# A sparse 3x3 convolution: one more load up front, a first store that waits for loads, and 28 matmuls on zeros in place of 12

## The chip, the core and the metric

One core of one Trainium2 chip. The metric is device time in microseconds (us) of one execution. The kernel before takes 127.04 us (median of 3 runs, 126.94 to 127.04; its profiled run 127.33). The span in a profile, from the first to the last instruction, is about 1.7 us shorter than the time. Each run is sorted by state, fast or slow, and only fast runs are compared.

## The reference, cut to what matters

```python
# x: (16, 64, 64, 64) fp32, weight: (128, 64, 3, 3) fp32, 90% zeros; output: (16, 128, 64, 64) fp32
x_pad = np.pad(x, ((0, 0), (0, 0), (1, 1), (1, 1)), mode='constant')
for b, co, ci, kh, kw:                     # five nested loops
    if weight[co, ci, kh, kw] != 0:
        output[b, co] += weight[co, ci, kh, kw] * x_pad[b, ci, kh:kh+h, kw:kw+w]
```

Input x is 16.8 MB, the output is 33.6 MB, the weights are 0.3 MB.

## The kernel before

Two images form a pair: their 64 input channels each fill 128 partitions, and there are eight pairs. A pair's load casts fp32 to bf16 on the way and is issued from GpSimd; a pair's output goes out in two stores of 2 MB, issued from SyncE. The first half of pair 0 comes as fp32 and is cast on chip (the head). TensorE runs small matmuls on zeros while it has nothing else to do, so that its clock does not fall.

```python
    nc.sync.dma_start(out=w_sb, in_=weight.rearrange("o i kh kw -> o (i kh kw)"))
    x_head = o_pool.tile([128, H, W], FP32, name="o")
    nc.sync.dma_start(out=x_head[:, 0:HEAD, :], in_=pair(0)[:, 0:HEAD, :])
    nc.gpsimd.dma_start(out=xs[0][:, HEAD:H, :], in_=pair(0)[:, HEAD:H, :])
    ...                                              # (cut)
    EARLY = 4
    for p in range(1, EARLY):
        load(p)                                      # pairs 1, 2, 3 up front
    ...
    keep_busy(27)                                    # 128x128 matmuls on zeros
    ...                                              # casts and transposes of the weights
    keep_busy(12)
    ...
    for p in range(NP):
        o = [o_pool.tile([C_OUT, H, W], FP32, name="o") for _ in range(2)]
        for blk in range(4):
            ...                                      # 30 matmuls, 4 additions on VectorE, 2 copies on ScalarE
                if p > 0 and blk == 1 and p + EARLY - 1 < NP:
                    load(p + EARLY - 1)              # pairs 4 to 7
        if not last:
            for n in range(2):
                nc.sync.dma_start(out=out[2 * p + n], in_=o[n])
```

## Time and profile before

| what | kernel before |
|---|---|
| time, median | 127.04 us |
| span of the profiled run (127.33 us) | 125.6 us |
| first product of TensorE; last addition of VectorE ends | 7.43 us; 113.66 us |
| first store issued; pair 6's first store issued | 23.5 us; 100.3 us |
| the two data queues' packets | 97.0% of 16 engines' span |
| HBM traffic | 17.07 MB read, 33.55 MB written |

How to read it: the page divides the span into 40 slices of 3.14 us and gives the busy share of each engine in tenths.

### The profile page before, as it was taken

What the parts mean: (1) busy time and instruction counts of PE and PEld (TensorE: products, weight loads), DVE (VectorE), ACT (ScalarE), POOL (GpSimd) and SP (SyncE); (2) the same over time, 40 slices, a digit from 0 to 9 for tenths busy, and PEclk for the clock granted to TensorE, in tenths of its full rate; (3) what the DMA queues carried; (4) which work ended last, traced back from release to release, by engine and by line L of the source; (5) the groups of instructions that cost most, each with busy time, mean ns of one, the idle gap of its engine ahead of it and who ended that gap; (6) DMA issues with size and microseconds to landing.
All of it is one profiled execution on the core that took longest, in us unless ns stands there. A gap on an engine that the chain in (4) does not pass through costs nothing.

```text
span 125.6 us, 2510 instructions
## 1 busy us (share of the span) xinstructions
PE 109.4 (87%) x1014; PEld 56.1 (45%) x1014; DVE 82.3 (66%) x135; ACT 39.0 (31%) x71; POOL 40.6 (32%) x45
## 2 busy tenths in 40 slices
PE   6769999999999999999999999999999999970000
PEld 6624444545454545444554555455545555430000
DVE  0352477877787777888788878877877787772000
ACT  4541533333333333333333333333333333330000
POOL 6327353334433443334333333333333330000000
PEclk9967999999999999999999999999999999999555
DMA  4999999999999999999999999999999999999980
GB/s 119 361 230 214 214 209 219 217 157 399 423 334 305 303 433 311 344 308 407 342 305 329 397 428 444 418 420 423 438 428 444 418 423 423 433 405 423 431 373 26
DMA packets 4044, 42.93 MB, mean 342 GB/s; under 512 B 448, under 2 KB 448, under 8 KB 704
## 3 DMA queue, kind: packets, MB, share of 16 engines
q1 hardware_dynamic: 2880, 34.90, 66.1%
q0 software_dynamic: 1152, 7.86, 30.9%
q8 instruction: 8, 0.13, 0.4%
q14 instruction: 4, 0.03, 0.1%
HBM read 17.07 MB, written 33.55 MB: 403 GB/s over the span
## 4 chain that ended last, share of the span: by engine, by line
PE 83%; DMA 5%; DVE 1%; issue 1%; DVEq 0%; SPq 0%
PE ps L146 83%; DMA o<-in_x_dram 5%; DVE o L179 1%; DVEq L229 0%; DVE x L97 0%; SPq L60 0%; DVEq L179 0%
## 5 line engine op out<-in xcount | busy, mean ns | idle before, releaser
L179 DVE TENSOR_TENSOR o<-ps,pc 128x512 f32<-128x512 f32 x124 | 77.8, 686 | 22.1 <-PE ps L146 19.8
L146 PE MATMUL ps<-x,wT 64*128 64x504 bf16 (+3 forms) x780 | 90.1, 378 | 1.5 <-DVE x L97 1.5
L146 PEld LDWEIGHTS <-wT 64*128 64x128 bf16 x966 | 52.1, 95 | 54.0 <-issue 3.4
L165 POOL TENSOR_TENSOR s<-x 128x512 bf16<-128x512 bf16 x31 | 35.6, 1151 | 59.7 <-PE ps L146 43.3
L172 ACT COPY pc<-ps 128x512 f32<-128x512 f32 x62 | 33.3, 589 | 64.0 <-issue 61.8
L146 PE MATMUL ps<-s,wT 64*128 64x512 bf16 (+1 forms) x186 | 25.5, 377 | 0.0
L82 PE MATMUL ps<-idle_rhs 128*128 128x128 bf16 x39 | 3.9, 283 | 1.0 <-DVE idle_rhs L77 1.0
L82 PEld LDWEIGHTS <-idle_rhs 128*128 128x128 bf16 x39 | 3.5, 133 | 1.0 <-DVE idle_rhs L77 1.0
L68 POOL DMA_DIRECT2D x<-in_x_dram x7 | 3.9, 559 | 0.0
L160 DVE COPY o<-ps 128x512 f32<-128x512 f32 x2 | 1.4, 692 | 3.6 <-PE ps L146 3.6
L101 DVE CAST w_bf<-w_sb 128x192 bf16<-128x192 f32 (+1 forms) x4 | 1.1, 345 | 2.8 <-DMA w_sb<-in_weight_dram 2.8
L159 ACT COPY o<-ps 128x512 f32<-128x512 f32 x2 | 1.2, 586 | 4.0 <-PE ps L146 4.0
L97 ACT CAST x<-o 128x576 bf16<-128x576 f32 (+1 forms) x2 | 1.5, 802 | 1.2 <-DMA o<-in_x_dram 1.2
L97 DVE CAST x<-o 128x576 bf16<-128x576 f32 x1 | 0.5, 460 | 2.0 <-DMA o<-in_x_dram 2.0
L101 ACT ACT_TABLE_LOAD x1 | 1.3, 1283 | 0.7 <-PEq L218 0.7
L101 ACT CAST w_bf<-w_sb 128x64 bf16<-128x64 f32 (+1 forms) x2 | 0.7, 416 | 1.7 <-DMA w_sb<-in_weight_dram 1.7
L107 PE MATMUL ps<-ident,w_bf 128*128 128x128 bf16 x9 | 0.9, 222 | 0.3 <-DVE w_bf L101 0.3
L111 DVE TENSOR_TENSOR wT<-ps,wT 128x384 bf16<-128x384 f32 x2 | 1.0, 550 | 0.0
L63 POOL DMA_DIRECT2D x<-in_x_dram x1 | 0.7, 691 | 0.8 <-POOLq L218 0.8
L107 PEld LDWEIGHTS <-w_bf 128*128 128x128 bf16 x9 | 0.5, 97 | 0.8 <-DVE w_bf L101 0.7
L77 DVE MEMSET idle_rhs<- 128x64 uint32 x1 | 0.1, 112 | 0.8 <-PEq L218 0.8
L122 DVE CAST wT<-ps 128x384 bf16<-128x384 f32 x1 | 0.6, 552 | 0.0
(8 smaller groups left out, 1.9 us busy)
## 6 DMA issues: line engine op xcount, KB each, us to landing
out_dram<-o SPq DMA_DIRECT2D x14, 2048.0 KB, 16.9
x<-in_x_dram POOLq DMA_DIRECT2D x7, 1024.0 KB, 15.5
out_dram<-o SPq DMA_DIRECT2D x4, 1024.0 KB, 10.6
o<-in_x_dram SPq DMA_DIRECT2D x1, 1024.0 KB, 5.7
x<-in_x_dram POOLq DMA_DIRECT2D x1, 512.0 KB, 7.5
w_sb<-in_weight_dram SPq DMA_DIRECT2D x1, 288.0 KB, 3.0
```

Of the source, the lines that this page charges most:

```text
L68: nc.gpsimd.dma_start(out=xs[p], in_=pair(p))
L82: nc.tensor.matmul(idle_ps, idle_rhs, idle_rhs, start=True, stop=True)
L97: copy(out=xs[0][:, a:b, :], in_=x_head[:, a:b, :])
L101: copy(out=w_bf4[:, g, a:b, :], in_=w_v[:, k : k + b - a, :])
L107: nc.tensor.matmul(wps[:, j, :], src, ident, start=True, stop=True)
L111: nc.vector.tensor_tensor(out=wT[:, g], in0=wps, in1=wT[:, G1], op=SUB)
L146: nc.tensor.matmul(ps[n][:, lo:hi, c_lo:c_hi], tap(g, kw, n), src[q, a:b:step, c_lo + kw - 1 : c_hi + kw - 1], start=(i == 0), stop=(i == ...
L159: nc.scalar.copy(out=o[0][:, r0 : r0 + rows, :], in_=ps[0])
L160: nc.vector.tensor_copy(out=o[1][:, r0 : r0 + rows, :], in_=ps[1])
L165: nc.gpsimd.tensor_tensor(out=s, in0=xs[p][:, r0 : r0 + 16 : 2, :], in1=xs[p][:, r0 + 1 : r0 + 16 : 2, :], op=ADD)
L172: nc.scalar.copy(out=c, in_=shared[n])
L179: nc.vector.tensor_tensor(out=o[n][:, first : r0 + 16 : 2, :], in0=ps[n], in1=pc[n], op=ADD)
```

## The change

Its intent: have x on chip early, keep stores out of the way of the first loads, and close the pause of TensorE before the first products.

```diff
-    EARLY = 4
-    for p in range(1, EARLY):
-        load(p)
+    EARLY = 5
+    landed = [load(p) for p in range(1, EARLY)][-2]
 ...
-    keep_busy(12)
+    keep_busy(28)
 ...
-                if p > 0 and blk == 1 and p + EARLY - 1 < NP:
-                    load(p + EARLY - 1)
+                if p > 1 and blk == 1 and p + EARLY - 2 < NP:
+                    load(p + EARLY - 2)
 ...
-                nc.sync.dma_start(out=out[2 * p + n], in_=o[n])
+                st = nc.sync.dma_start(out=out[2 * p + n], in_=o[n])
+                if p == n == 0:
+                    tc.add_manual_dep(st.ins, landed.ins.name, ...)   # (arguments cut) wait for pair 3
```

`landed` is the load of pair 3, the fourth pair. (The load function also takes a range of rows now, which no call uses.)

More of the change, by code (lines that the diff above doesn't have):

```diff
@@ L65, with load @@
     make_identity(nc, ident)
-    def load(p):
-        nc.gpsimd.dma_start(out=xs[p], in_=pair(p))
-    EARLY = 4
-    for p in range(1, EARLY):
-        load(p)
+    def load(p, a=0, b=H):
+        return nc.gpsimd.dma_start(out=xs[p][:, a:b, :], in_=pair(p)[:, a:b, :])
+    EARLY = 5
+    landed = [load(p) for p in range(1, EARLY)][-2]
     idle_rhs = const_pool.tile([128, 128], BF16, name="idle_rhs")
@@ L202 @@
             for n in range(2):
-                nc.sync.dma_start(out=out[2 * p + n], in_=o[n])
+                st = nc.sync.dma_start(out=out[2 * p + n], in_=o[n])
+                if p == n == 0:
+                    tc.add_manual_dep(
+                        st.ins,
+                        landed.ins.name,
+                        mybir.DependencyInfo(
+                            mybir.DependencyClass.Sync, mybir.DependencyReason.DATA
+                        ),
+                        reason="loads first",
+                    )
 _INS = ['x', 'weight']
```

## The prediction

> **What bounds the kernel now.** I read the chain of work that ended last first, because it names the wrong suspect, and then the page's slices and DMA queues.
>
> ```profile
> PE 83%; DMA 5%; DVE 1%; issue 1%; DVEq 0%; SPq 0%
> ...
> PE   6769999999999999999999999999999999970000
> ...
> PEclk9967999999999999999999999999999999999555
> DMA  4999999999999999999999999999999999999980
> ...
> q1 hardware_dynamic: 2880, 34.90, 66.1%
> q0 software_dynamic: 1152, 7.86, 30.9%
> ```
>
> The chain gives TensorE 83%, but it stops at the last compute instruction. A slice is 3.14 us. TensorE is done after slice 35 (111 us, the last VectorE addition 113.7 us), while DMA stays at 9 to slice 37, so something other than compute fills the last 12 us of 125.6. The two data queues together took 66.1% + 30.9% = 97.0% of 16 engines' span, 121.8 us. Only 3.8 us are left, for the start and the end.
>
> Next I asked for stretches. The columns after the engines are granted TensorE clock, DMA share and GB/s.
>
> ```profile
> 24.00:26.00 2.00, 2.00 (x22) 1.03 (x20) 1.40 (x4) 0.44 (x1) 0.62 (x1) 1.00 1.15 205
> 26.00:28.00 2.00, 2.00 (x22) 0.96 (x18) 1.27 (x3) 1.07 (x2) 1.15 (x1) 1.00 0.93 131
> 28.00:32.00 4.00, 4.00 (x40) 2.02 (x38) 3.27 (x6) 1.07 (x2) 1.66 (x2) 1.00 1.00 391
> ...
> 76.00:100.00 24.00, 24.00 (x228) 12.00 (x226) 19.06 (x31) 7.52 (x14) 8.07 (x7) 1.00 1.00 425
> 100.00:116.00 16.00, 12.30 (x116) 5.95 (x112) 10.90 (x18) 4.29 (x8) 1.15 (x1) 1.00 1.00 424
> 116.00:121.00 5.00, 0.00 (x0) 0.00 (x0) 0.00 (x0) 0.00 (x0) 0.00 (x0) 0.55 1.01 428
> 121.00:122.00 1.00, 0.00 (x0) 0.00 (x0) 0.00 (x0) 0.00 (x0) 0.00 (x0) 0.50 0.80 336
> ```
>
> From 76 to 121 us the engines move 424 to 428 GB/s without a gap, also after TensorE has stopped: the stores have a backlog. The loads at 205 GB/s are not slow: a load is counted by what it writes in bf16, half of what it reads in fp32, so 205 to 217 written is 410 to 434 read. The one thin place is 26 to 28 us, 131 GB/s, at full DMA share. The DMA records there show load packets of 8 KB taking 1.0 to 1.3 us where they take 0.625 us everywhere else; their excess from 24 to 30 us, over 16 engines, is 1.1 us. It begins about 2 us after the first store was issued (23.5 us), and store packets appear only at 27.7 us.
>
> The backlog shows in the stores' own answer, here the two last ones, issued at 113.1 and 113.7 us:
>
> ```profile
> L200 SPq DMA_DIRECT2D out_dram<-o x2: 332/678/1023, 113.1 to 113.7; - x2
> ...
> DMA to landing us min/median/max: 8.9/9.8/10.7
> ```
>
> A megabyte at 425 GB/s needs 2.5 us; these take about 10, so they stand behind some 6 or 7 us of earlier stores. I take the bound to be the DMA engines, with TensorE ahead by that much.
>
> **What the Trainium skill says.** "DMA: Bandwidth & Descriptors", section Bandwidth, puts the fabric ceiling at 435.2 GB/s; the 424 to 428 here are 98% of it, so there is no rate to win by ordering. The same page, "Issuing engines are not separate DMA queues", says that transfers from all issuers run on the same 16 engines and interleave. The trace agrees: from 36 to 46 us, with a load and a store in flight, both together reach the 330 GB/s or so that half-and-half of 210 and 425 gives (336). "TensorE: Matmul & The Clock Gate", Part 1, says that an idle TensorE falls to half clock and that activity is judged in windows of about 3.4 us. The trace agrees: after a pause of 1.53 us the granted clock is 0.50 from 7.3 to 10.7 us, one such window. "Perfetto Trace Analysis", What "DMA-bound" means, counts the individual DMA engines as one of the things that can bind; the steady 16 engines at work here are that case.
>
> **The change, part by part.**
>
> *28 for 12 matmuls on zeros.* In the timeline:
>
> ```profile
> 5.06 0.83 PE L82 MATMUL ps<-idle_rhs 128*128 128x128 bf16 x12
> ...
> 7.43 5.57 PE L146 MATMUL ps<-x,wT 64*128 64x512 bf16 x36 [1.53 <-DVE x L97]
> ...
> 13.48 2.77 PE L146 MATMUL ps<-x,wT 64*128 64x512 bf16 x24
> ...
> 23.50 0.88 SPq L203 DMA_DIRECT2D out_dram<-o  x2
> ```
>
> Twelve take 0.83 us, of which the last one's own 0.22 us is latency: 0.61 / 11 = 0.055 us apart. The 28th starts at 5.06 + 27 x 0.055 = 6.56 and ends near 6.8 us, before the first product can start at 7.43 (it waits for the cast of x, and that for the head load). So they cost nothing and shrink the pause from 1.53 to about 0.65 us. If that keeps the clock full, the 36 first products, 5.40 us from 7.43 to 12.83, run at the later spacing, 24 from 13.48 to 16.07 us or 0.108 us each: 36 x 0.108 = 3.9 us. TensorE and all behind it is 1.5 us earlier: VectorE ends near 112.2 us.
>
> *The fifth pair up front.* Its load is issued at about 4 us in place of 18.16 us, one more issue of 0.57 us on GpSimd, which idles 4.4 us right after. But loads stand in line on one queue: the fourth pair's landed at 24.1 us (3.5 + 20.6). The fifth was already queued by then in the kernel before, and its packets began when the fourth's ended. It starts landing at the same moment either way.
>
> *Three loads come later.* The loop now issues pair p + 3 in block 1 of pair p from p = 2 on: pairs 5, 6, 7 at pairs 2, 3, 4. In the kernel before, p + 3 from p = 1 on put the same pairs at the same places. So nothing moves but 1.5 us of clock; the last lands near 72 us and is needed near 98 us.
>
> *The first store's wait.* Without it the store would move from 23.5 to 22.0 us. With it, it waits for the fourth pair, 24.1 us, and is 0.6 us later than before. Meanwhile the engines have the fifth pair, 1.05 MB or 4.9 us at 214 GB/s, of which some 0.2 MB is done by 24.0 us: work until about 28 us, and longer if the dip repeats. Store packets came 4.2 us after issue before; 24.1 + 4.2 = 28.3 us. It just about covers: between 0 and 0.6 us of idle engines. Output buffers: the next use of the first store's buffer is in pair 3, at about 52 us, and it landed at 35.4 us; no stall.
>
> Sum on the path that sets the end: bytes the same, 0; TensorE's 1.5 us go into backlog, 0; store start 0 to +0.6; the dip 0 to -1.1 with its repetition far likelier. I take -0.1: 127.04 becomes about 126.9 us.
>
> **Rivals.** *TensorE is the bound after all.* The chain's 83% speaks for it; then 1.5 us come off and the time is 125.5 us. Against it: the last stores take 10 us for 2.5 us of bytes, and DMA share is full to 121 us. *The dip goes.* If it comes from stores breaking into the fourth load, the wait removes it: 127.04 - 1.1 = 125.9 us. For: it starts after the first store. Against: the slow packets are mostly the fifth pair's, which still overlaps. *The engines run dry* around 28 us before the first store gets going: up to +0.6, and the same dip on top if its length is fixed, 127.6 us. *GpSimd holds up TensorE* with a longer issue list: its first addition starts at 8.51 us and waits for a cast, with 4.4 us idle ahead; I see nothing there. *The slowest engine* sets the end: the last store's 16 completions spread over 2.5 us (121.4 to 123.9), so a different split of the dip over engines can shift the end by a few tenths.
>
> **Range and chances.** Runs of one kernel agree within 0.1 us. The downward rival of 1.1 and the upward one of 0.6 are each under one in four, so 126.1 to 127.5 us should hold it 8 times in 10. Two per cent is 2.5 us. Faster by that needs almost all of the 3.8 us in which the engines were not full; slower needs them idle for 2.5 us with loads queued. Chances: faster 0.03, same 0.94, slower 0.03.
>
> **What would show it.** Right: granted clock 1.00 from 7 to 11 us and the first products in about 3.9 us; first store issued near 24.1 us; again some 424 GB/s to about 121 us; last stores issued near 112.2 us and taking some 11 us to land, 1.5 us longer than before; the dip again near 26 to 29 us. Wrong: the last stores take under 8 us (then no backlog, and compute decides), a stretch of DMA share under 0.8 between 24 and 30 us, or no dip, which would give up to 1.1 us.

## The result

The first measurement gave 127.34 us (median of 4 runs with a slow one among them, 127.22 to 131.02; the fast runs 127.16 to 127.44) against 127.04 us, ratio of fast runs 1.0018, 95% interval 1.0001 to 1.0035. A second one on another chip, called a1_again below, gave 127.09 us (6 runs, 126.96 to 127.19) against 127.05 us, ratio 0.999, interval 0.9967 to 1.0013. The time is the same. A ratio here is the mean time of one kernel's fast runs over that of the other's from the same rounds, so it is not quite the ratio of the medians quoted beside it. Executions over 1.5% slower than the fastest of the same kernel are left out of the means.

The first measurement's profiled execution fell in the slow state (131.02 us, span 129.3 us). In it the head landed near 11 us and compute started 4.4 us late. The kernel before has such runs too (129.57, 129.27 and 130.23 us; 3 of the 22 executions in rounds c and d below), so I read nothing of the change from it. All that follows is from the fast profile of a1_again, which is the same kernel.

Its page, the lines that answer to those of before:

```profile
PE   6999999999999999999999999999999999930000
...
PEclk9999999999999999999999999999999999998555
DMA  4999999999999999999999999999999999999980
...
q1 hardware_dynamic: 2880, 34.90, 66.2%
q0 software_dynamic: 1152, 7.86, 30.7%
...
PE 81%; DMA 5%; DVE 1%; issue 1%; DVEq 0%; SPq 0%
```

TensorE fills three tenths of the 36th slice where it filled seven, and the clock row no longer falls in its third and fourth slices (that stretch at half clock is called the dent below). The DMA row is the same to the digit, the packets and bytes of the queues are the same, and their shares differ by 0.2 at most.

Its timeline, the matmuls on zeros and the first products, then the first stores and the first load from inside the loop (start, duration):

```profile
5.32 2.00 PE L82 MATMUL ps<-idle_rhs 128*128 128x128 bf16 x28
7.39 3.99 PE L146 MATMUL ps<-x,wT 64*128 64x512 bf16 x36
11.19 0.83 PE L146 MATMUL ps<-s,wT 64*128 64x512 bf16 x6
...
24.25 0.82 SPq L203 DMA_DIRECT2D out_dram<-o  x2
...
29.33 0.57 POOL L68 DMA_DIRECT2D x<-in_x_dram  x1
```

The 28 matmuls end at 7.32 us, just ahead of the first product at 7.39. The 36 products take 11.19 - 7.39 = 3.80 us where they took 5.40. Everything in the loop that follows TensorE is 1.6 us earlier: the load is issued at 29.33 us and was at 30.96; the last addition ends at 112.02 us and was at 113.66.

The stretches of both kernels around the first products show why (the granted clock is the third number from the end). Before:

```profile
7.40:11.00 3.60, 3.57 (x20) 1.56 (x21) 1.37 (x3) 1.03 (x2) 2.49 (x3) 0.54 1.08 224
```

After, with the stretches that the prediction read:

```profile
7.40:11.00 3.60, 3.60 (x36) 1.93 (x36) 2.02 (x4) 1.57 (x3) 2.53 (x3) 1.00 1.06 221
24.00:26.00 2.00, 2.00 (x22) 1.08 (x20) 1.49 (x3) 1.07 (x2) 1.02 (x1) 1.00 1.05 221
26.00:28.00 2.00, 2.00 (x22) 1.08 (x20) 1.79 (x3) 0.00 (x0) 0.14 (x1) 1.00 1.08 193
28.00:30.00 2.00, 2.00 (x22) 1.04 (x19) 1.27 (x3) 1.08 (x2) 1.67 (x2) 1.00 0.90 356
...
76.00:100.00 24.00, 24.00 (x230) 12.83 (x226) 18.48 (x31) 8.60 (x16) 9.23 (x8) 1.00 1.01 431
100.00:116.00 16.00, 10.67 (x100) 5.47 (x96) 9.85 (x16) 3.23 (x6) 0.00 (x0) 0.97 1.00 422
116.00:121.00 5.00, 0.00 (x0) 0.00 (x0) 0.00 (x0) 0.00 (x0) 0.00 (x0) 0.50 1.01 426
121.00:122.00 1.00, 0.00 (x0) 0.00 (x0) 0.00 (x0) 0.00 (x0) 0.00 (x0) 0.50 0.62 262
```

The engines move the same 422 to 431 GB/s until 121 us, although TensorE has stopped earlier. So the 1.6 us must be waiting in the stores, and they are. The two last ones:

```profile
L200 SPq DMA_DIRECT2D out_dram<-o x2: 333/677/1021, 111.5 to 112.0; - x2
...
DMA to landing us min/median/max: 10.3/11.2/12.1
```

They are issued 1.6 and 1.7 us earlier than before and take 1.4 us longer to land: the later landing is 112.0 + 12.1 = 124.1 us, and was 113.7 + 10.7 = 124.4 us.

### The profile page after: what moved, and what is told of

It reads as the page before. It is cut to its first block, busy times and chain, and to the rows that moved or that the text cites. A ratio compares the mean times of both kernels' runs of the same rounds, so it can differ in the third digit from the quotient of the medians.

```text
span 129.3 us, 2542 instructions
## 1 busy us (share of the span) xinstructions
PE 111.6 (86%) x1030; PEld 58.2 (45%) x1030; DVE 82.3 (64%) x135; ACT 39.0 (30%) x71; POOL 40.7 (31%) x45
## 4 chain that ended last, share of the span: by engine, by line
PE 81%; DMA 8%; DVE 1%; issue 1%; DVEq 0%; SPq 0%
PE ps L146 81%; DMA o<-in_x_dram 8%; DVE o L179 1%; DVEq L238 0%; DVE x L97 0%; SPq L60 0%; DVEq L179 0%
## 5 line engine op out<-in xcount | busy, mean ns | idle before, releaser
L146 PEld LDWEIGHTS <-wT 64*128 64x128 bf16 x966 | 52.7, 95 | 57.0 <-issue 7.1
L82 PE MATMUL ps<-idle_rhs 128*128 128x128 bf16 x55 | 5.1, 276 | 1.0 <-DVE idle_rhs L77 1.0
L82 PEld LDWEIGHTS <-idle_rhs 128*128 128x128 bf16 x55 | 4.8, 130 | 1.0 <-DVE idle_rhs L77 1.0
L120 ACT CAST wT<-ps 128x384 bf16<-128x384 f32 x1 | 0.5, 479 | 0.3 <-PE ps L107 0.3
```

The costliest lines, as they stand in the source:

```text
L82: nc.tensor.matmul(idle_ps, idle_rhs, idle_rhs, start=True, stop=True)
L146: nc.tensor.matmul(ps[n][:, lo:hi, c_lo:c_hi], tap(g, kw, n), src[q, a:b:step, c_lo + kw - 1 : c_hi + kw - 1], start=(i == 0), stop=(i == ...
```

## The experiments

Theory: the 16 DMA engines bind (at the rate that they get from memory; no run here separates the two), all they have to do stays the same, and compute's gain goes into the backlog of stores. Rivals: TensorE and what follows it bind; the first store's wait or the meeting of stores and loads costs or saves engine time. Twelve kernels ran. "Dry" below is a stretch in which the engines had nothing to do.

| run | edit | median us | ratio to the kernel before |
|---|---|---|---|
| a1_again | the changed kernel | 127.09 | 0.999 |
| a2_only28 | before, 28 matmuls | 127.01 | 0.9987 |
| a3_no_gate | changed, no wait | 127.02 | 0.9987 |
| a4_12 | changed, 12 matmuls | 127.27 | 1.0004 |
| b1_one_store_less | before, one 2 MB store left out | 124.65 | 0.9796 |
| b2_fewer_matmuls | before, fewer matmuls | 126.34 | 0.9929 |
| b3_all_first | changed, all loads first, store waits for the last | 129.75 | 1.0219 |
| c1_all_queued_gate6 | the same, store waits for the seventh pair | 127.42 | 1.0031 |
| c2_all_queued_no_gate | the same, no wait | 127.34 | 1.0025 |
| c3_after_store_less | changed, one 2 MB store left out | 124.52 | 0.980 |
| d1_four_less_12 | before, four 2 MB stores left out | 125.72 | 0.984 |
| d2_four_less_28 | the same, 28 matmuls | 124.17 | 0.9771 |

Runs of one letter shared a chip and their runs of the kernel before, whose medians were 127.05 (a), 127.12 (b), 127.07 (c) and 127.18 us (d). The runs with stores left out, and b2, give wrong results. The medians of b1, b2 and d1 have one slow run in them.

### Do the engines bind? Fewer matmuls, and one store less

```diff
 # b2: in pairs 2 to 7
         todo = [(t, kw) for t in terms for kw in KW_ORDER]
+        if cut:
+            todo = todo[:4]          # 4 of 6 in each product on x
 # b1: the kernel before
-            for n in range(2):
+            for n in range(1 if p == 3 else 2):
```

> The kernel before with a third of the matmuls on x left out in pairs 2 to 7 (8 of 24 per block; result wrong on purpose), all additions, copies, loads and stores kept. TensorE's block falls from 3.2 to about 2.4 us, and VectorE's 4 x 0.686 = 2.7 us sets its pace: compute should end some 10 us earlier. If the DMA engines bind, the time stays at 127.0 within 0.3 us; if TensorE binds, it falls by at least 5 us.

> The kernel before without one of its 2 MB stores (the second half of pair 3), so its result is wrong on purpose; all compute stays. If the DMA engines bind, 2.1 MB at 427 GB/s come off: 4.9 us, so 122.1 us. If TensorE and what follows it bind, nothing comes off (127.0 us).

b2 took 126.24 us on average in its fast runs (126.05 to 126.50), ratio 0.9929. The end of its chain of work, then what SyncE waited for at the end, before and in b2, and one wait of VectorE in b2 (total, times, longest):

```profile
98.38 0.60 DVEq L231
98.98 0.60 DVE o L181
```

```profile
SPq L229 <- DMA out_dram<-o: 9.5, 4, 2.4
...
SPq L231 <- DMA out_dram<-o: 22.8, 4, 15.6
...
DVE o L181 <- DMA out_dram<-o: 4.7, 1, 4.7
```

VectorE is done at 99.58 us, 14.1 us earlier than in the kernel before, and the time falls by 0.9 us. The rest of the gain is spent by SyncE in waiting for stores, 22.8 us where it was 9.5. VectorE even stood still for 4.7 us, until a store had freed one of the seven output buffers: here the stores hold up compute. The 0.9 us are more than the 0.3 us that I allowed. By the DMA records b2's last store packet ends at 122.8 us, 1.1 us earlier than in the kernel before, but what ends it earlier is not settled. Against 14 us the verdict is plain: TensorE and VectorE are not what ends this kernel.

b1 took 124.54 us on average in its fast runs (124.32 to 124.67; its profiled run was slow and is not used), 2.6 us less than the 127.12 beside it. The 4.9 us of engine time that I took out did not all come back. So the engines bind, but compute is close behind them. The next run shows where it takes over.

### Where compute takes over: one store less in the changed kernel

```diff
-            for n in range(2):
+            for n in range(1 if p == 3 else 2):
                 st = nc.sync.dma_start(out=out[2 * p + n], in_=o[n])
```

> The changed kernel without one 2 MB store of pair 3 (result wrong on purpose), as was done to the kernel before, where the time fell to 124.5 us and not to 122.1, since the engines then went dry and compute bound. If the matmuls on zeros really bring compute forward by 1.6 us and the engines hide it, it shows here: about 123.0 us. If the time is 124.5 us again, the clock gains nothing on the path of compute either, or the kernel before had it in its fast runs too (their granted clock was 0.96 to 0.97, as in the changed kernel).

124.52 us, all five runs between 124.39 and 124.74. Its stretches late in the run:

```profile
94.00:96.00 2.00, 2.00 (x22) 1.03 (x19) 1.96 (x4) 0.63 (x2) 0.53 (x1) 1.00 1.04 434
96.00:98.00 2.00, 2.00 (x22) 1.12 (x20) 1.31 (x3) 0.44 (x1) 0.61 (x1) 1.00 0.52 221
98.00:100.00 2.00, 2.00 (x24) 1.09 (x20) 1.41 (x3) 1.07 (x2) 1.15 (x1) 1.00 0.35 147
100.00:102.00 2.00, 2.00 (x22) 1.07 (x20) 2.00 (x4) 0.31 (x1) 0.00 (x0) 1.00 1.15 483
```

Between 96 and 100 us the engines are about half idle, some 2 us in sum: all stores of pairs 0 to 5 are out and pair 6 is not yet computed. Its first store is issued at 98.6 us. From there on 8.4 MB (pairs 6 and 7) need 19.7 us at 427 GB/s whatever came before, and that sets the end. So the cushion between the DMA bound and the compute bound is what came off here, 2.6 us, and not 4.9.

The time is that of b1 again, so the matmuls on zeros did not show. The likely reason is the granted clock: b1's fast runs had 0.962 to 0.972, c3's 0.960 to 0.968, so the kernel with 12 seems to have kept its clock in those runs. No fast run of b1 has a profile, so this is inferred. The pair d was made to see it apart.

### What the 28 matmuls are worth when nothing hides them

```diff
 # d1: the kernel before; d2: the same with keep_busy(28)
-            for n in range(2):
+            for n in range(1 if 2 <= p <= 5 else 2):
```

> The kernel before, 12 matmuls on zeros, without the second store of each of pairs 2 to 5 (8.4 MB or 19.6 us of engine time less; result wrong on purpose), so that the engines have no backlog and compute paces the end. Theory: the end is then the issue of pair 6's stores plus its own and pair 7's 8.4 MB, 19.7 us, some 122 us of span, and each us of compute counts. Where the granted clock falls to half after 7 us, the run is 1.5 us longer than where it does not; fast runs near 124.5 us or near 126 us by that. If DMA still bound, it would be below 115 us.

> The same with 28 matmuls on zeros. Theory: the clock stays full (as in all six profiles of fast runs with 28 so far), so its runs sit near 124.4 us, and it is up to 1.5 us faster than the same with 12, less where those kept their clock too. This is what the 28 are worth when nothing hides them. If they are worth nothing in themselves, both agree within 0.2 us.

The fast runs, one by one:

| run | mean granted clock | time, us |
|---|---|---|
| d1, 12 matmuls | 0.956 | 125.82, 125.62, 125.85 |
| d1, 12 matmuls | 0.971 | 124.31, 124.56 |
| d2, 28 matmuls | 0.963 to 0.971 | 124.31, 125.38, 124.19, 124.00, 124.16, 124.04 |

With 12 there are two groups, 125.76 and 124.44 us on average, and the clock tells them apart: one stretch of 3.41 us at half clock lowers the mean by 3.41 x 0.5 / 123 = 0.014, and they are 0.015 apart. With 28, five of six runs lie at 124.0 to 124.3 us; the sixth, 125.38, has a full clock and stays unexplained. (d1's profiled run was slow, 128.62 us, and is left out.) So 28 matmuls are worth about 1.6 us (125.76 against 124.14, without that sixth run) in the executions where 12 lose the clock. In the others it is 0.3 us, or 0.1 with the sixth run, which two runs of d1 can't tell from nothing. In the fast profiles the dent was there in 2 of 3 with 12 matmuls (the kernel before and a4, not b2) and in none of the seven with 28 whose first product started by 8.3 us. It was there in the eighth with 28, b3, which the expectation of d2 overlooked: its first product started at 10.20 us, 2.69 us after the last matmul on zeros, and the granted clock was 0.50 from 9.69 to 13.1 us. So the 28 kept the clock only where the head came in time.

The pair also sizes the cushion: compute-paced runs are at 124.2 us with a full clock and 125.8 us with the dent, the real kernels near 127.05 us. The engines hide 1.3 us for the kernel before when it has the dent, and 2.9 us otherwise.

### Twelve or 28, wait or no wait, in the whole kernel

```diff
 # a2: the kernel before          # a4: the changed kernel      # a3: the changed kernel
-    keep_busy(12)                 -    keep_busy(28)            -                if p == n == 0:
+    keep_busy(28)                 +    keep_busy(12)            +                if False:
```

> The changed kernel again, to have a profile of its fast state and to see how often it is slow. If the DMA engines bind, its fast runs stay within 0.3 us of the kernel before, the granted clock is 1.00 from 7 to 11 us, compute ends 1.5 us earlier (the last VectorE addition near 112.2 us instead of 113.7) and the last stores take about 1.5 us longer to land. If TensorE binds, the end moves with it and the fast runs are 1.5 us shorter. A slow run should again show one DMA engine some 3 us behind from the start and the head load landing near 11 us.

> The kernel before with 28 instead of 12 matmuls on zeros and nothing else. DMA-bound theory: same time as before within 0.2 us, first store issued at 22.0 us instead of 23.5. The rival that TensorE binds: 125.5 us. If stores that start while the fourth load is still landing cost something, as the author of the wait must have thought, this is a few tenths slower than before.

> The changed kernel without the wait of the first store. If the wait costs idle engines (rival: they run dry before the first store gets going), this is up to 0.6 us faster than the changed kernel. If the wait is neutral, they agree within 0.15 us. If the wait does save something, this is slower than the changed kernel.

> The changed kernel with only 12 matmuls on zeros. DMA-bound theory: within 0.2 us of the changed kernel, with the granted clock at half for one window after 7 us as in the kernel before, and compute ending 1.5 us later than in the changed kernel. The rival that TensorE binds: 1.5 us slower than the changed kernel.

127.09, 127.01, 127.02 and 127.27 us, with the kernel before at 127.05 beside them. a4 is 0.2 us above a1, the sign that a lost clock would give, but its profile also starts its first product 1.0 us later (8.42 us, a late head), so I do not give it to the clock. The others agree within 0.1 us. Among them a2 and a3 differ only in the loads (the fifth up front), and are at 127.01 and 127.02 us: that load changes nothing either. The wait does hold the first store; what SyncE waited for in a1 (total, times, longest):

```profile
SPq L203 <- DMA x<-in_x_dram: 22.6, 1, 22.6
```

The store is issued at 24.25 us with the wait and at 21.68 us in a3 without it, and neither the one nor the other changes the end. Both rivals fall: the wait costs nothing, and it saves nothing.

### The thin place near 26 us, and loads strictly first

```diff
 # b3 (the changed kernel)                       # c1: [-2]     # c2: [-2], and "if False:" for the wait
-    EARLY = 5
-    landed = [load(p) for p in range(1, EARLY)][-2]
+    EARLY = 8
+    landed = [load(p) for p in range(1, EARLY)][-1]
```

> The changed kernel with all seven whole-pair loads issued up front and the first store waiting for the last of them, so that no store runs beside a load (result right). Loads should have landed near 42 us, then 33.55 MB of stores at 427 GB/s take 78.6 us: last bytes near 122 us. If the thin place at 26 to 28 us is the price of stores and loads running side by side for the first time, it is gone and the time is about 126.0 us, 1 us below the kernel before. If it is a price of the first store in any company, it moves to 42 us and the time is 127.0 us or, with the first store's start-up unhidden, 128 us.

b3 is 2.6 us slower, beyond each of its forecasts. (Its profiled run took 130.57 us, the longest of four; the head was late in it, as said above, which doesn't touch what follows here.) By its DMA records there is no slow packet where its stores begin, but this:

```profile
40.00:42.00 2.00, 2.00 (x22) 1.04 (x20) 2.00 (x4) 0.08 (x1) 0.02 (x1) 1.00 0.96 201
42.00:44.00 2.00, 2.00 (x22) 0.99 (x19) 1.27 (x3) 1.00 (x2) 1.15 (x1) 1.00 0.18 37
44.00:46.00 2.00, 2.00 (x22) 0.98 (x18) 1.76 (x3) 0.84 (x2) 0.73 (x1) 1.00 0.58 242
```

In the DMA records the median engine has finished its loads at 42.3 us, the slowest at 44.0. The wait is for the slowest; the store is issued at 44.44 us and its first packet comes at 45.29. By the records the engines stand dry for 2.7 us in all. So the thin place needs stores and loads together: here the first store alone brought no slow packets (one profile). It also shows what a wait costs once no load lies behind it. In the changed kernel the fifth load lies there, and its wait is free.

> All loads up front as in the run before, but the first store waits for the seventh pair, not the eighth, so that its start-up lies beside the last load. Slow packets where stores and loads meet cost engine time (0.65 to 1.1 us in the runs so far), and the engines running dry cost 2.7 us in the run that waited for the last load. Here the meeting is short (some 3 us of load left when the first store packet comes): if the loss is the meeting itself, whatever its length, 0.7 us of slow packets and no dry stretch, 127.0 us; if the loss grows with the overlap, about 126.4 us. If the engines still run dry, over 127.5 us.

> All loads queued up front and no wait at all: stores meet loads from 22 us on and share the engines until about 62 us, one single meeting. DMA-bound theory: same bytes, no dry stretch, one loss of 0.7 us: 127.0 us within 0.3. The rival that running loads and stores side by side lowers the rate as long as it lasts: slower than the kernel before by 0.5 us or more, since they overlap for 40 us instead of four times 10.

c1 and c2 have no dry stretch, and come out at 127.42 and 127.34 us, 0.3 us above the kernel before, which is neither of the figures that their theories gave. The excess of slow load packets (time over 0.624 us each, summed, over 16 engines) was 0.33 us in c1 and 0.67 in c2, against 1.13 in the kernel before and 0.65 in a1. It does not grow with the overlap: c2's stores and loads share the engines from 26 to some 62 us, at 321 GB/s from 36 to 60 us, which is the half-and-half of 214 and 427. But less excess did not make these kernels faster. In both, the last store packet ends at 124.0 us and a1's at 123.7, while the median engine is done at 121.5 (c1), 122.2 (c2) and 121.9 us (a1). So the slowest engine decides the end, and why it is 1.8 to 2.5 us behind the median (1.3 us in the kernel before) is not settled. Nor is it settled what makes the packets slow where stores and loads meet.

No version beat the two kernels: a2 and a3 are within 0.1 us of the kernel before.

## Why the prediction was right, and where it was not

The forecast was 126.9 us (126.1 to 127.5) with 94% for no change; the medians are 127.34 and 127.09 us. The spread was taken too small: fast runs of one kernel were said to agree within 0.1 us, and those of the kernel before lay between 126.86 and 128.23 us. By its own steps:

- **The bound.** Right. Compute 14 us earlier is worth 0.9 us (b2), a store less is worth 2.6 us (b1, c3).
- **28 matmuls cost nothing and give 1.5 us to TensorE.** Right for the profiles at hand: 3.80 us for the first products where 3.9 was forecast, the end of compute at 112.02 where it said 112.2. The 28 took 2.00 us rather than 1.74 and still fit. The prediction says that the trace agrees with the page on the clock; it does on the 3.4 us at half clock, but not on the 1.53 us of pause that led to it (see the last section). What the step did not know: the kernel before loses its clock in some executions only (d1), so for the typical run the gain is smaller than the one that its profile shows.
- **The fifth pair lands when it landed before.** Right: issued at 4.1 us it took 27.3 us, so 31.4 us, against 18.2 + 13.8 = 32.0.
- **The later loads stay in place but for the clock.** Right: 29.33 for 30.96 us.
- **The first store's wait, 0 to 0.6 us.** Issued at 24.25 us (24.1 forecast), cost nothing (a3).
- **The dip repeats.** Right in kind, smaller in this profile: 193 GB/s from 26 to 28 us instead of 131, an excess of 0.65 us instead of 1.1. The sum let the dip count in full towards the time (0 to -1.1 us), and that was not shown: with an excess 0.5 us smaller the time was the same, and c1 with 0.33 us was not faster. Profiles of kernels on either side range from 0.56 to 1.13 us at that place in fast runs, so I do not give the difference to the change.
- **"They stand behind some 6 or 7 us of earlier stores. I take the bound to be the DMA engines, with TensorE ahead by that much."** This is the term that was mis-sized. The cushion is 1.3 to 2.9 us (d1, d2, c3). The fault is in the step from the queue's length to a lead: I took the last store's landing of about 10 us, subtracted its own 2.5 us and called the rest lead. But what stands ahead of it are pair 6's stores and the first half of pair 7, which compute itself had released only from 100.3 us on. With the last two stores these are 8.4 MB, which need 19.7 us at any rate, and end near 120 us before any delay. The verdict stood because the change only moves compute further ahead, and for that any lead above zero will do.
- **Slips on which nothing rests.** The half-and-half of 210 and 425 GB/s is 318, not "330 or so"; the 336 is what was measured from 36 to 46 us. TensorE ends at 112.3 us, not 111. And 2.5 us are two thirds of 3.8, not "almost all".
- **The rival that the dip goes** and the rival that **the engines run dry** did not come about in the fast profile of the changed kernel; the second did in b3.

## What to carry to other kernels

Before working on an engine's clock or its waits, look at what is still at work after the last compute instruction; if that is a steady DMA row at its full rate, earlier compute turns into later landings. To learn how far compute is ahead, take one transfer out and see how much of its time comes back: the length of the queue at the end overstates it, since the last transfers belong to compute's own last results. A wait that puts loads first was free here while another load lay behind the one waited for (a1); where none did, the kernel was 2.6 us slower (b3).

## What the Trainium skill lacked or had wrong

- "TensorE: Matmul & The Clock Gate", Part 1, gives the idle state "after" an idle window of about 3.4 us and advises against idle gaps longer than that. Here a pause of 1.53 us before the first product was enough for half clock from 7.3 to 10.7 us in the kernel before, while pauses of 0.78 (c1), 0.85 (c2) and 1.35 us (b2) kept the clock. So its rule for gaps was too generous here. What went with the loss was how busy TensorE was in one whole window: where windows of 3.41 us begin can be read from the times at which the clock records change. TensorE was busy for 50% (before, from 3.86 us), 42% (a4, from 5.95) and 36% (b3, from 6.28) of the window that ended when the clock fell, and for 60% (b2, from 4.50), 75% (c2, from 4.75) and 77% (c1, from 6.35) where it was kept. That is no threshold: at the end of a4 a window with 47% kept the clock. The page also says that the window runs free of the kernel's start. The position of the windows differed between these runs, which fits a clock that is lost in some executions of d1 and kept in others.
- "DMA: Bandwidth & Descriptors", "Issuing engines are not separate DMA queues", says that transfers interleave. It does not say that where stores first meet loads, load packets can take 1.0 to 1.3 us (before; single ones up to 1.9 in a4) instead of 0.625, 0.6 to 1.1 us of engine time in all, and that the first store's first packet then comes 2.9 to 4.3 us after issue, against 0.85 us with no load beside it (b3).
